# Multiplying the first two column tiles of the input projection together, feature tile by feature tile, with eight matmuls on zeros ahead

## The chip, the cores and the metric

The kernel runs on one core of a Trainium2 chip. The metric is the device time of one execution in microseconds (us). Besides the TensorE (PE in the profile; PEld is its weight load) a core has VectorE (DVE), ScalarE (ACT), GpSimd (POOL) and SyncE (SP), which here only issues DMAs. The engines run in parallel, each through its own list of instructions in order.

## What is computed

One layer of a hybrid decoder for 1024 positions of width 1024, in f32: RMSNorm, one input projection whose columns feed three kinds of token mixer (sparse attention, a gated convolution, gated linear attention), one output projection, a SwiGLU feed-forward part, a gated per-layer embedding, and a last norm. The part that the change touches is the projection, and of its columns the 512 of the convolution:

```
h = rms_norm(x, mix_norm_g[i])                      # x / rms(x) * g
z = h @ w_in[i]
(nq, kc, vc, ks_, vs_, kw, vw, ng, cu, gq, gk, gv, ga, gr) = jnp.split(z, split_at, axis=-1)
y_conv = conformer_conv(cu, ...)
def conformer_conv(u, w_dw, b_dw, ln_g, ln_b):
    a, g = jnp.split(u, 2, axis=-1)
    h = a * jax.nn.sigmoid(g)                       # then a causal convolution of 31 taps, norm, silu
```

## The kernel before

**Products.** TensorE computes in a shorter format than f32. Each f32 operand is therefore split into a high part (`hi`, written by ScalarE) and the rest (`lo`, written by VectorE or GpSimd), and each product is three matmuls: hi by hi, hi by lo, lo by hi.

**Operands of the projection.** `hT[hf][kt]` is the transposed input times the gain `g`, for half `hf` (512 positions) and feature tile `kt` (128 features, 8 tiles). `load_xT(hf)` loads 256 KB per tile and issues the two splitting instructions (L324 on ScalarE, L325 on VectorE). A tile of 128 output columns takes 512 KB of weights: `fetch(i)` calls `load_split`, one DMA into `nat` (L307), one cast into `whi` on ScalarE (L310) and one subtraction into `wlo` (L267). Here `whi` holds the eight 128x128 blocks of a column tile side by side.

**The tile product.** `mproj(i, hf, o)` goes over the eight feature tiles and issues the three matmuls of each (L368, L371, L372), 24 for one column tile and one half of the positions. `mtile(i)` does both halves, 48 matmuls, into two PSUM banks that the ring `early` gives out: tile 0 has banks 0 and 1, tile 1 banks 2 and 3, tile 2 banks 4 and 5, and tile 3 banks 0 and 1 again. So tile 3 has to wait until tile 0 has been read.

**What reads tile 0.** The norm's factor 1/rms per position is multiplied in after the product. `norm_x(hf)` loads x once more (8 loads of 512 KB), sums squares on ScalarE (L350), GpSimd forms the factors as diagonals `dg`, one matmul per half (L342) spreads them over the partitions, and ScalarE copies them into `rbc` (L343). Only then can VectorE read tile 0: `sg` = tile 0 by `rbc` (`scaled`, L355). `glu_tile(c)` goes on with a sigmoid of `sg` on ScalarE (L410, with a table load ahead), `sg` by `rbc` on GpSimd (L411), and `glu` = tile 1 by `sg` on VectorE (L414). The second call does the same with tiles 2 and 3. The taps of the convolution (L437, some 1.3 us each) follow on VectorE.

**After the four tiles** come row tiles: `row_tile` multiplies 128 positions by 384 columns of `w_a` (L398 to L400), then by 272 columns of `w_b`, for gated linear attention. Their weights pass through the same `load_split`. Later come tile 4, the chain of gated linear attention (`gla_ops`), attention, the output projection, and the feed-forward part.

**What sets the order.** The order in each engine's list is that of a scheduler which is given the program and simulates it with a cost table, and the places of the buffers in SBUF come from a dry pass of the same kind. So a change at the start can move instructions of any later part. SP issues a DMA only when the eighth DMA before it on SP has landed.

Of the kernel before, what the change touches and what calls it, by code (L numbers as in the profile page):

```python
# [10 lines left out]
F32R = mybir.dt.float32r  # L11
# [9 lines left out]
P = 128  # L21
NT = S // P
KT = D // P
# [195 lines left out]
def tile_block(ctx: ExitStack, tc: tile.TileContext, a: dict, out: bass.AP, plan: Plan):  # L219
    nc = tc.nc  # L220
    mm = nc.tensor.matmul
# [5 lines left out]
    banks = psum.tile([P, 8, 512], F32, name="banks")  # L227
# [11 lines left out]
    def B(name, dt=F32, shape=(P, 1024)):  # L239
        return place(name, shape, dt)  # L240
# [20 lines left out]
    low, high, early = Ring(0, 4), Ring(4, 8), Ring(0, 6)  # L261

    def f(ap):
        return ap.bitcast(F32)

    def sub(eng, o, i0, i1):
        return eng.tensor_tensor(out=o, in0=i0, in1=i1, op=ALU.subtract)  # L267
# [35 lines left out]
        return r  # L303

    def load_split(src, width=1024, lo_eng=None):
        nat = B("nat")
        nc.sync.dma_start(out=nat[:, :width], in_=src)  # L307
        hi = B("whi", F32R)
        lo_ = B("wlo", F32R)
        nc.scalar.copy(hi[:, :width], nat[:, :width])  # L310
        sub(lo_eng or nc.vector, lo_[:, :width], nat[:, :width], f(hi[:, :width]))
        return hi, lo_


    hT = [[], []]

    def load_xT(hf):
        for kt in range(KT):
            if kt % 2 == 0:
                xx = B("xT", F32, (P, 2, 512))  # L320
                for k in range(2):
                    nc.sync.dma_start(out=xx[:, k, :], in_=a["xT"][kt + k, :, hf * 512:hf * 512 + 512])
            x, o, g = xx[:, kt % 2, :], B("hT", F32R, (P, 2, 512)), pv["mixg"][:, kt:kt + 1]
            nc.scalar.activation(o[:, 0, :], x, AF.Copy, scale=g)  # L324
            nc.vector.scalar_tensor_tensor(out=o[:, 1, :], in0=x, scalar=g, in1=f(o[:, 0, :]), op0=ALU.mult,  # L325
                                           op1=ALU.subtract)
            hT[hf].append(o)
# [29 lines left out]
    ready = {}  # L357

    def fetch(i):
        if i < len(COL_T) and i not in ready:  # L360
            ready[i] = load_split(a["w_t"][i], lo_eng=nc.gpsimd if POOLLO[0] <= i < POOLLO[1] else None)

    def mproj(i, hf, o):
        hi, lo_ = ready[i]
        for kt in range(KT):
            w = slice(kt * P, (kt + 1) * P)
            x = hT[hf][kt]
            r = mm(o, hi[:, w], x[:, 0, :], start=kt == 0, stop=False)  # L368
            if kt == 0:
                behind("pe", r)  # L370
            mm(o, hi[:, w], x[:, 1, :], start=False, stop=False)  # L371
            mm(o, lo_[:, w], x[:, 0, :], start=False, stop=kt == KT - 1)  # L372

    def mtile(i):
        fetch(i)
        fetch(i + 1)
        ps = (early if i < 4 else low)(2)
        for hf in range(2):
            mproj(i, hf, ps[:, hf * 512:(hf + 1) * 512])
            for g, n in queue:  # L380
                pump(g, n)
        return ps
# [20 lines left out]

    glu = []

    def glu_tile(c):
        ps = mtile(2 * c)
        sg = B("sg")
        scaled(sg, ps)
        nc.scalar.activation(sg, sg, AF.Sigmoid)  # L410
        nc.gpsimd.tensor_tensor(out=sg, in0=sg, in1=rbc, op=ALU.mult)  # L411
        ps = mtile(2 * c + 1)
        h = B("glu")
        nc.vector.tensor_tensor(out=h, in0=ps, in1=sg, op=ALU.mult)  # L414
        glu.append(h)
# [84 lines left out]
        nc.scalar.activation(gr, pb[:, 16:272], AF.Silu, scale=rx[:, t:t + 1])  # L500
        nc.gpsimd.tensor_tensor(out=gr, in0=gr, in1=pv["gng"], op=ALU.mult)

    fetch(0)
    load_xT(0)
    fetch(1)
    load_xT(1)
    nc.sync.dma_start(out=cst[:, 0:P], in_=a["cst"][:, 0:P])
    fetch(2)
# [8 lines left out]
    wal = const.tile([17, P], F32, name="wal")  # L517
    nc.sync.dma_start(out=wal, in_=a["wal"])

    glu_tile(0)  # L520
    taps = conv_taps(0)
    pump(taps, 10)
    pump(loadA, 2)
# [14 lines left out]
    ps = mtile(4)  # L538
# [122 lines left out]
    for i in range(2):  # L661
        ps = mtile(5 + i)
# [54 lines left out]
    for t in range(NT):  # L717
        ps = row_tile(wV, 280, t)
# [871 lines left out]
```

## Time and profile before

| | |
|---|---|
| time, median of 3 runs (lowest to highest) | 1403.82 us (1403.34 to 1405.22) |
| the profiled execution: its time, its span | 1403.04 us, 1401.2 us |
| busy: PE, PEld | 1371.5 us (98%), 1160.7 us |
| busy: DVE, ACT, POOL | 1031.6 us (74%), 664.7 us (47%), 553.4 us (39%) |
| mean granted clock of TensorE | 0.995 of full |
| chain of work that ended last | PE 86%, DVE 7%, DMA 2% |

All times within the profile are counted from the start of the span. In an answer with instructions in order of time (a timeline) a row has its start, its duration, the engine, the source line, the operation, what it writes and reads, how many equal ones follow one another (x7), and in brackets how long the engine was idle ahead of it and what it waited for. Matmuls are pipelined, so that what one costs is the distance from its start to the next one's and not its duration.

### The profile page before, as it was taken

How to read it: one execution, taken by the hardware profiler on the slowest of the kernel's cores; microseconds unless marked ns; L12 is line 12 of the kernel's file. 1: busy time of each engine (PE TensorE's matmuls, PEld its weight loads, DVE VectorE, ACT ScalarE, POOL GpSimd, SP SyncE). 2: the span in 40 equal slices, each digit the busy share in tenths (PEclk: the TensorE clock that was granted, in tenths of full speed). 3: DMA queues.
4: the chain of work that ended last, by engine and by line, in shares of the span. 5: the costliest groups of instructions: out<-in, count | busy, mean ns of one | idle time of the engine just before them, and what ended most of it. 6: DMA issues, size and time to landing. Idle time of an engine off the chain costs nothing.

```text
span 1401.2 us, 19420 instructions
## 1 busy us (share of the span) xinstructions
PE 1371.5 (98%) x7080; PEld 1160.7 (83%) x7080; DVE 1031.6 (74%) x1870; ACT 664.7 (47%) x1290; POOL 553.4 (39%) x592
## 2 busy tenths in 40 slices
PE   8999999999999998999999999999999999999997
PEld 6898777889999997888878888888888788888886
DVE  3897457548999895558786777777789999897533
ACT  7331532246888885536433343333345344444532
POOL 3761443346888864101465665556510000000111
PEclk9999999999999999999999999999999999999999
DMA  9201013400000013541332222333357743521111
GB/s 362 75 16 40 11 54 102 148 23 4 6 9 5 5 33 107 181 149 40 120 113 92 81 99 102 109 113 113 105 194 264 259 152 111 178 78 66 69 39 46
DMA packets 55744, 135.68 MB, mean 97 GB/s; under 512 B 5413, under 2 KB 10207, under 8 KB 55647
## 3 DMA queue, kind: packets, MB, share of 16 engines
q1 hardware_dynamic: 55502, 134.42, 27.6%
q8 instruction: 55, 0.90, 0.3%
q14 instruction: 43, 0.34, 0.1%
q10 hardware_dynamic: 144, 0.01, 0.0%
HBM read 102.68 MB, written 31.73 MB: 96 GB/s over the span
## 4 chain that ended last, share of the span: by engine, by line
PE 86%; DVE 7%; DMA 2%; ACT 1%; issue 1%; POOL 1%; SPq 0%; POOLq 0%; DVEq 0%; ACTq 0%
PE banks L1435 13%; PE banks L1052 8%; PE banks L1051 8%; PE banks L1050 8%; PE banks L966 3%; PE banks L371 3%; PE banks L372 3%; PE banks L368 3%; PE banks L1010 2%; PE banks L1011 2%; PE banks L906 2%; PE banks L1151 2%; PE banks L1487 2%; PE banks L1486 2%; PE banks L1485 2%; PE banks L1152 2%
## 5 line engine op out<-in xcount | busy, mean ns | idle before, releaser
L1052 PE MATMUL banks<-op 128*128 128x512 f32 x616 | 237.8, 390 | 1.3 <-DVE op L267 1.3
L1051 PE MATMUL banks<-op 128*128 128x512 f32 x616 | 238.5, 390 | 0.0
L1050 PE MATMUL banks<-op 128*128 128x512 f32 x616 | 235.9, 390 | 0.6 <-ACT op L1039 0.3
L1435 PE MATMUL banks<-op 128*128 128x512 f32 x924 | 211.2, 389 | 2.5 <-ACT op L1039 1.7
L1435 PEld LDWEIGHTS banks<-op 128*128 128x128 f32 x924 | 173.2, 188 | 39.7 <-ACT op L1039 2.6
L1039 ACT CAST op<-nat 128x512 fp32r<-128x512 f32 x200 | 118.8, 621 | 180.4 <-DVE op L267 59.8
L267 DVE TENSOR_TENSOR op<-nat,op 128x512 fp32r<-128x512 f32 x196 | 152.7, 801 | 30.5 <-ACT op L1039 30.1
L301 POOL TENSOR_SCALAR rsr<-ss 128x1 f32<-128x1 f32 x16 | 5.9, 369 | 339.8 <-ACT sq L1454 261.9
L1052 PEld LDWEIGHTS banks<-op 128*128 128x128 f32 x616 | 115.6, 188 | 26.4 <-DVE op L267 2.1
L1050 PEld LDWEIGHTS banks<-op 128*128 128x128 f32 x616 | 115.6, 188 | 25.8 <-ACT op L1039 0.7
L1051 PEld LDWEIGHTS banks<-op 128*128 128x128 f32 x616 | 115.6, 188 | 24.2 <-issue 0.5
L267 DVE TENSOR_TENSOR op<-ws,op 128x512 fp32r<-128x512 f32 x88 | 88.0, 1004 | 52.5 <-ACT op L1039 52.4
L921 POOL TENSOR_SCALAR p<-p,sums,gates 128x640 f32<-128x640 f32 (+7 forms) x128 | 100.9, 801 | 39.3 <-DVE sums L917 30.2
L912 ACT ACTIVATE p<-p,mn 128x640 f32<-128x640 f32 (+7 forms) x128 | 94.7, 742 | 13.3 <-DVE mn L909 13.2
L368 PE MATMUL banks<-hT,whi 128*128 128x512 f32 x208 | 84.6, 407 | 7.0 <-ACT hT L324 6.4
L1039 ACT CAST op<-ws 128x512 fp32r<-128x512 f32 x88 | 54.4, 622 | 76.9 <-PE banks L1052 45.5
L371 PE MATMUL banks<-hT,whi 128*128 128x512 f32 x208 | 83.9, 403 | 0.5 <-DVE hT L325 0.5
L372 PE MATMUL banks<-hT,wlo 128*128 128x512 f32 x208 | 82.6, 399 | 0.0
L966 PE MATMUL banks<-cst,p 128*128 128x128 f32 x448 | 71.2, 274 | 1.9 <-DVE pt L267 0.9
L906 PE MATMUL banks<-k,qst 128*128 128x512 f32 (+2 forms) x192 | 68.3, 361 | 0.9 <-POOL qst L267 0.5
L267 DVE TENSOR_TENSOR pt<-banks,pt 128x512 fp32r<-128x512 f32 (+1 forms) x114 | 64.1, 571 | 5.6 <-ACT pt L977 4.8
L1344 DVE TENSOR_TENSOR x<-banks,x 128x512 f32<-128x512 f32 x96 | 64.3, 683 | 5.3 <-PE banks L1435 5.0
(305 smaller groups left out, 3309.6 us busy)
## 6 DMA issues: line engine op xcount, KB each, us to landing
nat<-actd SPq DMA_DIRECT2D x33, 512.0 KB, 5.4
nat<-in_w_g SPq DMA_DIRECT2D x22, 512.0 KB, 3.3
nat<-in_w_u SPq DMA_DIRECT2D x22, 512.0 KB, 3.2
nat<-in_w_d SPq DMA_DIRECT2D x22, 512.0 KB, 5.4
nat<-in_w_t SPq DMA_DIRECT2D x13, 512.0 KB, 4.2
actd<-sg SPq DMA_DIRECT2D x22, 256.0 KB, 2.4
actd<-sa SPq DMA_DIRECT2D x11, 512.0 KB, 2.8
actd<-sg SPq DMA_DIRECT2D x11, 512.0 KB, 3.7
```

The costliest lines, as they stand in the source:

```text
L267: return eng.tensor_tensor(out=o, in0=i0, in1=i1, op=ALU.subtract)
L368: r = mm(o, hi[:, w], x[:, 0, :], start=kt == 0, stop=False)
L371: mm(o, hi[:, w], x[:, 1, :], start=False, stop=False)
L372: mm(o, lo_[:, w], x[:, 0, :], start=False, stop=kt == KT - 1)
L906: mark("pe", mm(ps[:, :max(w, 256)], q, kdup[br][g][:, k], start=True, stop=False))
L921: nc.gpsimd.tensor_scalar(out=ps_out[br][:, :n], in0=ps_out[br][:, :n], scalar1=sums[:, br:br + 1], scalar2=gates[:, qb, 3 * head(h) + 1 + ...
L966: nc.tensor.transpose(ps[:, (2 * m + e) * P:(2 * m + e + 1) * P], blk(e, kb, br, ka), ident)
L1039: nc.scalar.copy(o[:, 0, :], src)
L1050: mm(ps, w[:, 0, c], x[k][:, 0, :], start=start and k == 0, stop=False, skip_group_check=True)
L1051: mm(ps, w[:, 0, c], x[k][:, 1, :], start=False, stop=False, skip_group_check=True)
L1052: mm(ps, w[:, 1, c], x[k][:, 0, :], start=False, stop=k == 3, skip_group_check=True)
L1435: mm(groups[g][t], r[:, v, c], l[:, u, :], start=start and (i, u, v) == (0, 0, 0), stop=i == len(ops) - 1 and u == 1, skip_group_check=True)
```

## The change

Ahead of all else VectorE clears a tile of 128x512 (`warm`) and TensorE multiplies it eight times with itself into bank 7, which nobody reads. The weights of column tiles 0 and 1 are loaded and split in three cuts each (256, 256 and 512 columns, that is 2, 2 and 4 feature tiles), issued in turns with the loads of the features; the first two feature tiles keep a load each, the others come two at a time (512 KB). `first_tiles` then goes over the feature tiles and issues for each the three matmuls of column tile 0 and the three of column tile 1, first for one half of the positions and then for the other; `glu_tile(0)` takes both.

```diff
+    def split_parts(src, parts, lo_eng=None):
+        nat, hi, lo_ = B("nat"), B("whi", F32R), B("wlo", F32R)
+        for c in parts:
+            nc.sync.dma_start(out=nat[:, c], in_=src[:, c])
+            nc.scalar.copy(hi[:, c], nat[:, c])
+            sub(lo_eng or nc.vector, lo_[:, c], nat[:, c], f(hi[:, c]))
+            yield hi, lo_
...
-    def load_xT(hf):
+    def load_xT(hf, part=None):
         for kt in range(KT):
+            if hf == 0 and kt in (0, 2, 4):
+                part(0)
             if kt % 2 == 0:
                 xx = B("xT", F32, (P, 2, 512))
-                for k in range(2):
-                    nc.sync.dma_start(out=xx[:, k, :], in_=a["xT"][kt + k, :, hf * 512:hf * 512 + 512])
+                if hf == 0 and kt == 0:
+                    for k in range(2):
+                        nc.sync.dma_start(out=xx[:, k, :], in_=a["xT"][kt + k, :, hf * 512:hf * 512 + 512])
+                        if k == 0:
+                            part(1)
+                else:
+                    if hf == 0 and kt < 6:
+                        part(1)
+                    nc.sync.dma_start(out=xx, in_=a["xT"][kt:kt + 2, :, hf * 512:hf * 512 + 512].rearrange("k p j -> p k j"))
...
-    def mproj(i, hf, o):
+    def mproj(i, hf, o, kts=range(KT)):
         hi, lo_ = ready[i]
-        for kt in range(KT):
+        for kt in kts:
...
+    def first_tiles():
+        two = [early(2) for _ in range(2)]
+        for hf in range(2):
+            for kt in range(KT):
+                for i in range(2):
+                    mproj(i, hf, two[i][:, hf * 512:(hf + 1) * 512], [kt])
+        return two
+
-    def glu_tile(c):
-        ps = mtile(2 * c)
+    def glu_tile(c, two=None):
+        ps = two[0] if two else mtile(2 * c)
...
-    fetch(0)
-    load_xT(0)
-    fetch(1)
+    warm = B("warm", F32R, (P, 512))
+    nc.vector.memset(f(warm), 0.0)
+    for _ in range(8):
+        mm(banks[:, 7, :], warm[:, :P], warm, start=True, stop=True)
+    cuts = [slice(0, 256), slice(256, 512), slice(512, 1024)]
+    w01 = [split_parts(a["w_t"][i], cuts) for i in range(2)]
+
+    def part(i):
+        ready[i] = next(w01[i])
+
+    load_xT(0, part)
     load_xT(1)
...
-    glu_tile(0)
+    glu_tile(0, first_tiles())
```

The scheduler also moves instructions around this part. In the changed kernel the lines stand further down: L368, L371 and L372 are L380, L383 and L384, L342 is L354, L343 is L355, L355 is L367, L414 is L435, L437 is L458.

On TensorE, at the end of tile 2, the second matmul on `dg` stood six matmuls ahead of tile 3 before:

```order
140 L342 MATMUL banks<-dg 128x512 [waits Pool_49]
141 L368 MATMUL banks<-hT,whi 128x512
142 L371 MATMUL banks<-hT,whi 128x512
143 L372 MATMUL banks<-hT,wlo 128x512
144 L368 MATMUL banks<-hT,whi 128x512
145 L371 MATMUL banks<-hT,whi 128x512
146 L372 MATMUL banks<-hT,wlo 128x512
147 L368 MATMUL banks<-hT,whi 128x512 [waits DVE_49]
```

Now, at the same place, where the last row is again the first matmul of tile 3:

```order
144 L380 MATMUL banks<-hT,whi 128x512
145 L383 MATMUL banks<-hT,whi 128x512
146 L384 MATMUL banks<-hT,wlo 128x512
147 L354 MATMUL banks<-dg 128x512 [waits Pool_49]
148 L380 MATMUL banks<-hT,whi 128x512 [waits DVE_49]
```

The six matmuls that lay between the `dg` matmul and the wait for VectorE's read of tile 0 are ahead of both.

On ScalarE, from the second copy into `rbc` on, before (the casts of 816 columns are those of `w_b`):

```order
37 L343 COPY rbc<-banks 128x512 [waits PE_49]
38 L410 ACT_TABLE_LOAD
39 L410 ACTIVATE sg<-sg 128x1024 [waits DVE_49] x2
40 L310 CAST whi<-nat 128x816 [waits DMAHW1_49,Activation_49]
41 L310 CAST whi<-nat 128x816 [waits DMAHW2_49,DVE_49]
```

and now:

```order
40 L355 COPY rbc<-banks 128x512 [waits PE_49]
41 L313 CAST whi<-nat 128x768 [waits DMAHW5_49,Activation_49]
42 L313 CAST whi<-nat 128x816 [waits DMAHW6_49,Pool_49]
43 L431 ACT_TABLE_LOAD
44 L431 ACTIVATE sg<-sg 128x1024 [waits DVE_49] x2
45 L313 CAST whi<-nat 128x816 [waits DMAHW7_49,Activation_49]
```

Two casts have come between the copy and the sigmoids. The one of 816 columns waits for the first DMA of `w_b`, and that DMA waits for a matmul two places ahead of the second `dg` matmul.

On VectorE, from the first `glu` to the second, before:

```order
26 L414 TENSOR_TENSOR glu<-banks,sg 128x1024 [waits Pool_49]
27 L425 TENSOR_SCALAR banks<-glu,par 128x1024 [waits DMAHW6_49,DVE_49]
28 L437 SCALAR_TENSOR_TENSOR banks<-glu,par,banks 128x1023 [waits DVE_49]
29 L437 SCALAR_TENSOR_TENSOR banks<-glu,par,banks 128x1022 [waits DVE_49]
30 L437 SCALAR_TENSOR_TENSOR banks<-glu,par,banks 128x1021 [waits DVE_49]
31 L267 TENSOR_TENSOR wlo<-nat,whi 128x816 [waits DMAHW2_49,PE_49,Activation_49]
32 L414 TENSOR_TENSOR glu<-banks,sg 128x1024 [waits PE_49,Pool_49]
```

and now:

```order
30 L435 TENSOR_TENSOR glu<-banks,sg 128x1024 [waits Pool_49]
31 L446 TENSOR_SCALAR banks<-glu,par 128x1024 [waits DMAHW3_49,DVE_49]
32 L267 TENSOR_TENSOR wlo<-nat,whi 128x816 [waits DMAHW7_49,Activation_49]
33 L458 SCALAR_TENSOR_TENSOR banks<-glu,par,banks 128x1023 [waits DVE_49]
34 L267 TENSOR_TENSOR wlo<-nat,whi 128x816 [waits DMAHW6_49,DVE_49]
35 L458 SCALAR_TENSOR_TENSOR banks<-glu,par,banks 128x1022 [waits DVE_49]
36 L458 SCALAR_TENSOR_TENSOR banks<-glu,par,banks 128x1021 [waits DVE_49]
37 L458 SCALAR_TENSOR_TENSOR banks<-glu,par,banks 128x1020 [waits DVE_49]
38 L435 TENSOR_TENSOR glu<-banks,sg 128x1024 [waits PE_49,Pool_49]
```

One more subtraction and one more tap have come between the two. The second `glu` reads tile 3, and the row tile that starts 32 matmuls after the end of tile 3 goes into a bank of tile 3, in both kernels: it waits for the second `glu`.

## Rows read from the trace of the kernel before

**Rows 1.** The page: busy time of TensorE and the others, share of span.

```profile
PE 1371.5 (98%) x7080; PEld 1160.7 (83%) x7080; DVE 1031.6 (74%) x1870; ACT 664.7 (47%) x1290; POOL 553.4 (39%) x592
```

**Rows 2.** Waits of TensorE: who waited for whom, total us, times, longest us.

```profile
PE banks L1005 <- DVE att L996: 2.9, 2, 2.7
PE banks L616 <- POOL kd L577: 1.0, 1, 1.0
```

**Rows 3.** Timeline of TensorE, the first matmuls.

```profile
6.42 0.80 PE L368 MATMUL banks<-hT,whi 128*128 128x512 f32 x1 [6.42 <-ACT hT L324]
7.72 0.79 PE L371 MATMUL banks<-hT,whi 128*128 128x512 f32 x1 [0.50 <-DVE hT L325]
8.31 0.63 PE L372 MATMUL banks<-hT,wlo 128*128 128x512 f32 x1
...
11.72 0.43 PE L371 MATMUL banks<-hT,whi 128*128 128x512 f32 x1
12.00 0.40 PE L372 MATMUL banks<-hT,wlo 128*128 128x512 f32 x1
```

**Rows 4.** Timelines of ScalarE and VectorE, the first splits.

```profile
4.70 1.04 ACT L310 CAST whi<-nat 128x1024 fp32r<-128x1024 f32 x1 [2.26 <-DMA nat<-in_w_t]
5.65 0.72 ACT L324 ACTIVATE hT<-xT,par 128x512 fp32r<-128x512 f32 x1
...
5.78 1.23 DVE L267 TENSOR_TENSOR wlo<-nat,whi 128x1024 fp32r<-128x1024 f32 x1 [5.78 <-ACT whi L310]
6.92 5.38 DVE L325 SCALAR_TENSOR_TENSOR hT<-xT,par,hT 128x512 fp32r<-128x512 f32 x8
```

**Rows 5.** Windows: busy us (instructions) of PE, PEld, DVE, ACT, POOL; PEclk; DMA share; GB/s.

```profile
3.00:12.00 9.00, 5.08 (x12) 3.65 (x13) 6.22 (x9) 6.49 (x10) 0.20 (x1) 1.00 1.00 375
```

**Rows 6.** Timeline of TensorE around the two dg matmuls and tile 3.

```profile
35.09 0.40 PE L371 MATMUL banks<-hT,whi 128*128 128x512 f32 x1
...
41.70 1.02 PE L342 MATMUL banks<-dg 128*128 128x512 f32 x2
...
44.66 0.50 PE L368 MATMUL banks<-hT,whi 128*128 128x512 f32 x1 [0.54 <-DVE sg L355]
```

**Rows 7.** Timelines of ScalarE, GpSimd and VectorE, from the sigmoids to the second glu.

```profile
42.76 0.59 ACT L343 COPY rbc<-banks 128x512 f32<-128x512 f32 x1 [3.05 <-PE banks L342]
43.36 1.28 ACT L410 ACT_TABLE_LOAD   x1
44.66 2.17 ACT L410 ACTIVATE sg<-sg 128x1024 f32<-128x1024 f32 x2
46.73 0.86 ACT L310 CAST whi<-nat 128x816 fp32r<-128x816 f32 x1
...
45.79 5.55 POOL L411 TENSOR_TENSOR sg<-sg,rbc 128x1024 f32<-128x1024 f32 x2 [5.23 <-ACT sg L410]
...
48.99 1.21 DVE L414 TENSOR_TENSOR glu<-banks,sg 128x1024 f32<-128x1024 f32 x1
...
51.63 3.93 DVE L437 SCALAR_TENSOR_TENSOR banks<-glu,par,banks 128x1023 f32<-128x1023 f32 x3
55.70 1.10 DVE L267 TENSOR_TENSOR wlo<-nat,whi 128x816 fp32r<-128x816 f32 x1
56.73 1.21 DVE L414 TENSOR_TENSOR glu<-banks,sg 128x1024 f32<-128x1024 f32 x1
```

**Rows 8.** Timeline of TensorE, the first matmuls of the row tiles.

```profile
55.67 0.33 PE L398 MATMUL banks<-whi,hT 128*128 128x384 f32 x1
...
63.84 0.33 PE L400 MATMUL banks<-whi,hT 128*128 128x384 f32 x1
```

**Rows 9.** DMA issues from 40 to 60 us: times issued, KB, us to landing.

```profile
nat<-in_w_b SPq DMA_DIRECT2D x1, 272.0 KB, 3.5
```

**Rows 10.** Timeline of GpSimd in gated linear attention.

```profile
160.88 0.19 POOL L301 TENSOR_SCALAR rsc<-bmv 128x1 f32<-128x1 f32 x1
161.15 0.57 POOL L302 TENSOR_TENSOR rsc<-rsc,mhalf 128x1 f32<-128x1 f32 x1
```

**Rows 11.** Windows around two later stretches, columns as in rows 5.

```profile
531.80:534.00 2.20, 0.05 (x1) 0.00 (x0) 1.12 (x4) 2.20 (x6) 2.20 (x3) 1.00 0.00 0
534.00:537.40 3.40, 2.88 (x12) 2.79 (x13) 3.37 (x6) 1.96 (x6) 3.40 (x3) 0.50 0.01 2
```

More of the change, by code (lines that the diff above doesn't have):

```diff
@@ L305, in load_split @@
     def load_split(src, width=1024, lo_eng=None):
[L306 to L312, printed above, removed]
+        return list(split_parts(src, [slice(0, width)], lo_eng))[-1]
+    def split_parts(src, parts, lo_eng=None):
[5 more added lines that the diff above has]
+            yield hi, lo_
     hT = [[], []]
-    def load_xT(hf):
+    def load_xT(hf, part=None):
         for kt in range(KT):
+            if hf == 0 and kt in (0, 2, 4):
+                part(0)
             if kt % 2 == 0:
                 xx = B("xT", F32, (P, 2, 512))
-                for k in range(2):
-                    nc.sync.dma_start(out=xx[:, k, :], in_=a["xT"][kt + k, :, hf * 512:hf * 512 + 512])
+                if hf == 0 and kt == 0:
[7 more added lines that the diff above has]
+                    nc.sync.dma_start(out=xx, in_=a["xT"][kt:kt + 2, :, hf * 512:hf * 512 + 512].rearrange("k p j -> p k j"))
             x, o, g = xx[:, kt % 2, :], B("hT", F32R, (P, 2, 512)), pv["mixg"][:, kt:kt + 1]
@@ L411, in glu_tile @@
         nc.gpsimd.tensor_tensor(out=sg, in0=sg, in1=rbc, op=ALU.mult)
-        ps = mtile(2 * c + 1)
+        ps = two[1] if two else mtile(2 * c + 1)
         h = B("glu")
```

## The prediction

> **What bounds the kernel now.** I read the busy times first: TensorE is busy in 98% of the span, no other engine in more than 74% [rows 1]. So time is gained where TensorE starts, waits or runs at its lower clock, and hardly elsewhere. Next the waits of TensorE: two to remember are that for GpSimd's `kd` in gated linear attention, 1.0 us, and the longest after the start, 2.7 us in attention [rows 2]. Then its first matmuls in order of time. The first starts at 6.42 us, the second waits 0.50 us for VectorE, and from 8.31 to 11.72 us eight matmuls follow one another at 3.41 / 8 = 0.426 us; at 12.00 us the twelfth starts [rows 3]. Later, from 35.09 to 41.70 us, 29 matmuls of the same shape take 6.61 us, 0.228 each [rows 6]: the first eleven ran at about half rate, the lower of the clock's two levels (1.2 and 2.4 GHz).
>
> The change can thus win at two places: the time before the first matmul, and 0.2 us on each slow one. What it wins there must then get past the next places where TensorE waits for others.
>
> **The start.** Before, the first high part of the features (L324) stands behind a cast of 1024 columns (1.04 us), the first low part behind a subtraction of 1.23 us [rows 4]. Now a quarter of each stands there. With a cut at 0.3 to 0.4 us the first product can start 0.7 to 0.9 us earlier; I take 5.6 us. Its first matmuls, two of them on the high part alone, still wait once for VectorE, so I let the third start at 6.25 us and the rest follow.
>
> Do the data keep up? Half 0 needs 1 MB of weights and 2 MB of features, 3.15 million bytes. From 3 to 12 us the DMAs moved 375 GB/s [rows 5], which brings these by 3.0 + 8.4 = 11.4 us. The last pair of feature tiles costs VectorE 1.34 us more (8 in 5.38 us [rows 4]), so it is ready at about 13.3 us; TensorE, if at full rate, comes to its first at 6.25 + 34 x 0.228 = 14.0 us. It keeps up with 0.7 us to spare, because each tile now feeds six matmuls where it fed three. The additional instructions (four casts and subtractions, a memset, eight matmuls that end near 4.6 us) lie in time in which their engines had nothing else.
>
> A rule speaks against cutting loads. The Trainium skill, "DMA: Bandwidth & Descriptors", section Bandwidth, wants DMAs of 1 MiB or more for three quarters of the peak. Loads of 256 and 512 KB, eight in flight, gave the 375 GB/s of the row here, so the trace bears it out badly; at three quarters of that rate the same bytes would come 2.8 us later and TensorE would wait some 2 us in half 0.
>
> What does the clock do? **Unknown: whether eight matmuls on zeros lift it.** The trace has no such matmuls. Bounds: the clock is up when the real work starts, or it rises at 11.8 us as before. At the slow rate they occupy TensorE for 8 x 0.426 = 3.4 us, the real work follows a microsecond later, and the rise of before came 5.4 us after its first matmul, 4.1 after its second. The two stretches together look to me like the busy time that was followed by the rise, so I take the upper case. At 12.00 us TensorE is then at matmul 3 + 5.75 / 0.228 = 28 instead of 12: **16 x 0.228 = 3.65 us ahead**. In the lower case, 24 matmuls that would have started by 11.8 us are 12, and 2.6 us of that are gone.
>
> The Trainium skill, "TensorE: Matmul & The Clock Gate", Part 1, calls the slow state the default, which activity ends, and says that the number of slow matmuls at a start differs from run to run. No run here shows the second; it would put single runs between the two cases.
>
> **Tile 3.** The work up to the second `dg` matmul is else the same, but six matmuls that stood behind it are now ahead [the order rows of TensorE above]. Before, from the start of this matmul to the start of tile 3 went 44.66 - 41.70 = 2.96 us [rows 6]: spread, copy into `rbc` (42.76, 0.59), VectorE's read. These steps stay as they are, and cover is gone: the six, 1.36 us, are no longer hidden in it. Second `dg` matmul at 39.4 us (41.70 - 3.65 + 1.36), tile 3 at 42.36. **Lead left: 2.3 us.** GpSimd's `dg` cannot spoil it by much: squares and factors hang on the loads of x, whose bytes come as before, and 41.70 left them several us.
>
> **The second glu.** Here I expect most of the loss. ScalarE's sigmoids now stand behind the cast of the first `w_b` piece. Its DMA waits for a matmul 0.45 us ahead of the second `dg` matmul, 38.95 us. Its landing: one of 272 KB took 3.5 us among few others [rows 9]; this one has 408 KB and the DMAs to itself, and I take the same, thus 42.5, where the copy into `rbc` (1.65 us behind the `dg` matmul, as before) and the other cast are done at 41.9. Cast 0.86, table load 1.30, sigmoid 1.09, GpSimd's multiply 2.78 (5.55 for two) [rows 7] make 48.5 us for the first `glu`; before it was 48.99. Of the 2.3 us of lead only 0.5 have come through. From the first to the second `glu` went 56.73 - 48.99 = 7.74 us; one subtraction (1.10) and one tap (3.93 / 3 = 1.31) more stand between, 10.15. It starts at 58.7 and ends at 59.9 (1.21). TensorE needs this 32 matmuls behind tile 3: tile 3 ends 55.67 - 44.66 = 11.0 us after its start, at 53.4, and 32 at (63.84 - 55.67) / 47 = 0.174 [rows 8] make 58.9. **New wait: 1.0 us; lead left 1.3.** Before there was none: 55.67 + 5.6 = 61.2, against 57.9. What is queued behind it are the other row tiles, which would have been early by as much. Bounds: 0.4, if the DMA has landed by 41.9, and 2.3, if it takes over a microsecond longer than I say.
>
> **Gated linear attention.** GpSimd now does a pair on `rsc` (0.19 + 0.57 [rows 10]) ahead of its eight multiplies of `qb` and of `kd`, for which TensorE waited 1.0 us already. **0.76 us more**, between 0 (GpSimd was idle ahead of `qb`, and the pair may fit there) and 1.5.
>
> VectorE's taps in between don't count: a subtraction in them now waits for a late DMA, some 2 us, but VectorE was idle for 4.5 us behind its taps before it had to read tile 4. Attention and the output projection have a few other places in the order; I have no row that prices them, and the bounds are a wait of [rows 2] more or less. The feed-forward part has the same order.
>
> **Sum:** -3.65 + 1.36 + 1.0 + 0.76 = -0.53 us against the profiled 1403.04 (a span of 1401.2 and 1.8 around it), which is 0.8 below the median of the runs. Against the median: 1403.3. 0.2% of this is 2.8 us, which is about what a measurement of this kernel can tell from no change.
>
> **The rivals.**
>
> *The lead survives* (0.28). The `w_b` piece lands in time and `rsc` fits into GpSimd's idle time. Then 2.3 - 0.4 = 1.9 us stay: 1401.9 us, or down to 1400.9 where the first product also starts earlier than I say and some of VectorE's steps behind the first `glu` are quicker. For it: DMAs are few at 40 us. Against it: the DMA is issued only 3 us ahead of where its cast would have to start.
>
> *A wait of attention goes* (0.10). At 531.8 us TensorE is idle for 2.2 us and more, and behind this runs 3.4 us at a granted clock of 0.50 [rows 11], 1.7 us lost. If another order or a small shift removes both, 4.4 us are gained: 1399.4. Nothing in the change aims there.
>
> *The zeros don't lift the clock* (0.14). Then the work is done in the changed order at the slow rate up to 11.8 us, as if the warm matmuls weren't there: the lead is 1.05 - 1.36 = -0.3 at tile 3, and the waits behind it, which are counted from the second `dg` matmul, move along: 1403.3 + 2.6 = 1405.9.
>
> *The slower side: new idle time lets the clock fall* (0.10). Ahead of tile 3 TensorE now has nothing for 2.96 - 1.0 = 1.9 us, where it was idle for 0.54 [rows 6], and 1.0 us at the second `glu`. An idle time of 0.54 left the clock up; the one at 531.8, of 2.2 to 2.7 us, was followed by half rate [rows 2, 11]. It decides somewhere between. A drop of 3.4 us costs 1.7, which gives 1405.0; at both places 3.4: 1406.7.
>
> **How the numbers follow.** The forecast, a lead earned and spent, has 0.38, the rivals 0.28, 0.10, 0.14 and 0.10. The likeliest case alone lies in 1402.2 to 1404.6. For 8 in 10 I leave out the wait of attention below and the double drop of the clock above, and reach to a lead that survives almost whole, 1400.8, and somewhat past zeros that do nothing, 1406.4. Faster by over 0.2%, below 1401.0, is the wait of attention and 0.12 of the surviving lead, where other small waits go with it: 0.22. Slower, above 1406.6, is 0.07 of the last rival and 0.08 of the one on zeros, where a new wait in the moved order comes on top: 0.15. The rest is no change, 0.63.
>
> **What would show it.** The first real matmul at 5.4 to 5.9 us, and the third and later ones at 0.228 us, not 0.426. The second `dg` matmul near 39.4, tile 3 near 42.4, with an idle time ended by VectorE's `sg`. On ScalarE an idle time ahead of a cast of 816 columns that a DMA of `w_b` ends. A wait of TensorE for `glu` near 59 us, and a wait for `kd` of over 1 us near 160. The forecast is wrong if that wait for `glu` is missing, if matmuls at 0.426 reach to 11 us, or if a stretch behind 300 us has changed by more than the start has.

## The result, and the profile after

The changed kernel takes 1412.14 us (median of 6 runs, 1410.65 to 1415.74) where the kernel before took 1404.51 (6 runs beside them, 1401.22 to 1405.68): a ratio of 1.0064 (95% interval 1.0049 to 1.0078), 9 us slower by the ratio, and outside the forecast range. The profiled execution took 1413.79 us, with a span of 1412.0.

The busy time of TensorE and its waits, from the page and the view of waits (total us, times, longest):

```profile
PE 1380.1 (98%) x7088; PEld 1166.7 (83%) x7088; DVE 1035.3 (73%) x1875; ACT 665.9 (47%) x1294; POOL 551.9 (39%) x592
```
```profile
PE banks L410 <- DVE glu L435: 2.7, 1, 2.7
...
PE banks L380 <- ACT hT L336: 2.1, 1, 2.1
...
PE banks L380 <- DVE sg L367: 1.9, 1, 1.9
```

TensorE's busy time has risen by 8.6 us against [rows 1] for eight more matmuls of 0.43 us. So besides waits there is slower running. To see where, I follow one and the same matmul through the traces: its start is read in each, and the difference is how late TensorE stands there.

| start of | before | changed | later by |
|---|---|---|---|
| tile 3 | 44.66 | 45.76 | 1.10 |
| fifth row tile on `w_b` (its first L398) | 101.02 | 106.64 | 5.62 |
| first L748, key compression | 268.73 | 273.99 | 5.26 |
| first L1151, output projection | 537.10 | 543.54 | 6.44 |
| first L1050, feed-forward part | 638.56 | 646.38 | 7.82 |
| end of span | 1401.2 | 1412.0 | 10.8 |

More than half is there by 107 us. The first matmuls, in order of time:

```profile
1.43 3.78 PE L528 MATMUL banks<-warm 128*128 128x512 f32 x8 [1.43 <-DVE warm L526]
5.01 0.63 PE L380 MATMUL banks<-hT,whi 128*128 128x512 f32 x1
...
7.63 0.40 PE L380 MATMUL banks<-hT,whi 128*128 128x512 f32 x1
7.87 0.40 PE L384 MATMUL banks<-hT,wlo 128*128 128x512 f32 x1
...
9.03 0.39 PE L384 MATMUL banks<-hT,wlo 128*128 128x512 f32 x1
11.51 0.73 PE L380 MATMUL banks<-hT,whi 128*128 128x512 f32 x2 [2.09 <-ACT hT L336]
```

The first product comes at 5.0 us, earlier than the 5.6 of the forecast, and full spacing begins at 7.6, where the forecast had 6.25. The twelfth matmul starts at 9.03 us and not at 12.00 [rows 3], a lead of 3.0 us. Then TensorE stands still for 2.09 us, for the third feature tile, whose split on ScalarE itself waits for a load, and the next matmul, the thirteenth, leads by only 0.7 us (11.51 against 12.23):

```profile
10.73 1.33 ACT L336 ACTIVATE hT<-xT,par 128x512 fp32r<-128x512 f32 x2 [3.32 <-DMA xT<-in_xT]
```

Windows of the changed kernel (columns as in rows 5): from 3 to 12 us the DMAs moved 296 GB/s against 375 in [rows 5], and further down the five later stretches in which TensorE worked at a granted clock of 0.50:

```profile
3.00:12.00 9.00, 6.63 (x20) 4.29 (x18) 3.54 (x7) 4.12 (x9) 0.00 (x0) 1.00 0.87 296
65.50:68.80 3.30, 3.30 (x12) 3.30 (x11) 3.26 (x4) 0.00 (x0) 3.30 (x3) 0.50 0.26 66
297.60:304.30 6.70, 6.70 (x22) 5.47 (x22) 2.20 (x11) 3.81 (x12) 3.26 (x6) 0.50 0.00 0
461.40:464.70 3.30, 3.30 (x14) 3.11 (x14) 1.91 (x5) 0.16 (x1) 1.47 (x2) 0.50 0.00 0
539.90:546.70 6.80, 5.74 (x19) 4.97 (x20) 5.19 (x9) 3.55 (x9) 5.25 (x4) 0.50 0.00 1
1106.60:1109.80 3.20, 3.20 (x9) 2.42 (x9) 3.20 (x7) 0.62 (x1) 0.00 (x0) 0.50 1.04 401
```

The kernel before has such stretches only at 534 to 537 us [rows 11] and at 292 to 298:

```profile
291.70:298.50 6.80, 6.80 (x25) 5.86 (x25) 2.79 (x16) 4.44 (x13) 2.46 (x5) 0.50 0.00 0
```

In the changed one they add up to 24 us instead of 10, and half of the difference, some 7 us, is lost. The slow matmuls at the start are no part of this: there the column of the granted clock reads 1.00 in both kernels, also while matmuls follow one another at 0.426 us [rows 3, rows 5], so what is said here of the clock at the start is read from the spacing alone.

The largest new wait, from the `dg` matmul to the row tile, in the timelines of TensorE, ScalarE and VectorE:

```profile
42.81 1.02 PE L354 MATMUL banks<-dg 128*128 128x512 f32 x2
45.76 0.50 PE L380 MATMUL banks<-hT,whi 128*128 128x512 f32 x1 [1.93 <-DVE sg L367]
...
65.20 0.51 PE L410 MATMUL banks<-whi,hT 128*128 128x384 f32 x1 [2.68 <-DVE glu L435]
65.50 0.52 PE L411 MATMUL banks<-wlo,hT 128*128 128x384 f32 x1
...
68.95 0.34 PE L410 MATMUL banks<-whi,hT 128*128 128x384 f32 x1
69.12 0.33 PE L411 MATMUL banks<-wlo,hT 128*128 128x384 f32 x1
```
```profile
45.90 0.88 ACT L313 CAST whi<-nat 128x816 fp32r<-128x816 f32 x1 [0.72 <-DMA nat<-in_w_b]
```
```profile
51.65 1.23 DVE L435 TENSOR_TENSOR glu<-banks,sg 128x1024 f32<-128x1024 f32 x1 [3.95 <-POOL sg L432]
...
54.16 1.75 DVE L267 TENSOR_TENSOR wlo<-nat,whi 128x816 fp32r<-128x816 f32 x1
...
57.04 3.14 DVE L267 TENSOR_TENSOR wlo<-nat,whi 128x816 fp32r<-128x816 f32 x1
60.10 3.92 DVE L458 SCALAR_TENSOR_TENSOR banks<-glu,par,banks 128x1022 f32<-128x1022 f32 x3
63.92 1.22 DVE L435 TENSOR_TENSOR glu<-banks,sg 128x1024 f32<-128x1024 f32 x1
```

From 62.5 to 65.2 us TensorE waits for the second `glu`, and right behind it the matmuls follow at 0.32 us instead of 0.17 until 68.9: the granted clock has fallen to 0.50. The wait of 2.7 us and the some 1.7 that the slow stretch costs are, together, nearly all of the 4.5 us by which TensorE falls back between tile 3 and 107 us.

### The profile page after: what moved, and what is told of

It is laid out like the page before. It is cut to its first block, busy times and chain, and to the rows that moved or that the text cites. A ratio compares the mean times of both kernels' runs of the same rounds, so it can differ in the third digit from the quotient of the medians.

```text
span 1412.0 us, 19441 instructions
## 1 busy us (share of the span) xinstructions
PE 1380.1 (98%) x7088; PEld 1166.7 (83%) x7088; DVE 1035.3 (73%) x1875; ACT 665.9 (47%) x1294; POOL 551.9 (39%) x592
## 4 chain that ended last, share of the span: by engine, by line
PE 82%; DVE 9%; DMA 3%; ACT 2%; issue 2%; POOL 1%; SPq 0%; POOLq 0%; DVEq 0%; ACTq 0%
PE banks L1465 12%; PE banks L1082 8%; PE banks L1081 8%; PE banks L1080 8%; PE banks L996 3%; PE banks L383 3%; PE banks L384 3%; PE banks L380 3%; PE banks L1040 2%; PE banks L1041 2%; DVE op L267 2%; PE banks L936 2%; PE banks L1181 2%; PE banks L1183 2%; PE banks L1182 2%; PE banks L937 2%
## 5 line engine op out<-in xcount | busy, mean ns | idle before, releaser
L942 ACT ACTIVATE p<-p,mn 128x640 f32<-128x640 f32 (+7 forms) x128 | 94.7, 742 | 13.2 <-DVE mn L939 13.1
L380 PE MATMUL banks<-hT,whi 128*128 128x512 f32 x208 | 82.2, 403 | 4.3 <-ACT hT L336 2.1
L383 PE MATMUL banks<-hT,whi 128*128 128x512 f32 x208 | 83.9, 403 | 0.1
L384 PE MATMUL banks<-hT,wlo 128*128 128x512 f32 x208 | 82.5, 398 | 0.0
```

## The experiments

Each is told against runs of the kernel before on the same chip (medians 1403.0 to 1403.7 us).

**Zeros alone (warm_only).** The kernel before, with these lines ahead and the order else the same:

```diff
+    warm = B("warm", F32R, (P, 512))
+    nc.vector.memset(f(warm), 0.0)
+    for _ in range(8):
+        mm(banks[:, 7, :], warm[:, :P], warm, start=True, stop=True)
     fetch(0)
     load_xT(0)
```

> The kernel before, with the memset and the eight matmuls on zeros ahead and nothing else; the order of all other instructions is that of the kernel before. Theory A (the zeros lift the clock early, and what the changed kernel loses is lost by the loads and the moved order): matmuls at 0.228 us from 7 to 8 us on, the first tile then bound by the low parts of the features, tile 3 near 42.8 us instead of 44.66, no new wait behind it, a time 1 to 2.5 us below that of the kernel before. Theory B (a lead at the start is taken away by the waits of later stages, whatever the loads are): tile 3 as early, but the time within 0.7 us of before. Theory C (the matmuls on zeros are harmful in themselves, by the bank, the memset or the clock falling again): slower than before.

Measured: 1404.76 us (12 runs), ratio 1.0012 (0.9997 to 1.0027). No gain, and at the start none was possible in the profiled execution, since the full spacing began later than without zeros [rows 3]. It was the slowest of the twelve (1409.83 us); how the others started is not on record. Its matmuls:

```profile
12.83 0.56 PE L371 MATMUL banks<-hT,whi 128*128 128x512 f32 x1
13.23 0.40 PE L372 MATMUL banks<-hT,wlo 128*128 128x512 f32 x1
13.46 0.39 PE L368 MATMUL banks<-hT,whi 128*128 128x512 f32 x1
```

None of the three theories had such a late rise. Tile 3 starts at 45.23, 0.57 later than before.

**Eleven zeros (warm_11)**, `range(11)` in the same lines, so that no gap is left ahead of the first product:

> The kernel before with eleven matmuls on zeros instead of eight, which reach to 6.1 us, where the first product starts; order else as before. Theory D (eight didn't lift the clock because about a microsecond without work lay between them and the first product): the clock is up by 8.5 us, matmuls at 0.228 from there, tile 3 at 43 to 43.7, the time 0.5 to 1.5 us below that with eight. Theory E (where the clock rises is chance from run to run, zeros or not): a rise anywhere from 6 to 13 us, and a median within 0.7 us of the kernel before.

Measured: 1406.2 us (12 runs), ratio 1.0021 (1.0001 to 1.004). In its profile full spacing begins at 8.1 us and TensorE is 1.5 us ahead at 30 us, as D has it. But the order was not wholly that of before: the second `dg` matmul came directly ahead of tile 3, as in the changed kernel, and 1.93 us of waiting for `sg` took the lead away (tile 3 at 44.53).

**No zeros (no_warm)**, the changed kernel without the four lines above:

> The changed kernel without the memset and the matmuls on zeros; the order of the rest is that of the changed kernel. Theory A: the clock rises between 9 and 12 us; since the features are late anyway, TensorE waits for the third feature tile until about 11.5 us with or without the zeros, so that tile 3 starts at 45.8 to 47, the wait for the second glu of 2 to 3 us is still there, and the time is 1410 to 1414, within 2 us of the changed kernel. If instead the zeros carry what the change wins, it is 3 us or more slower than the changed kernel.

Measured: 1410.47 us (11 runs), ratio 1.004 (1.0026 to 1.0054): no slower than with zeros (1.0064 and 1.0051 in its two measurements). Without them TensorE runs at half rate until 9.5 us, and still comes to the missing feature tile early:

```profile
9.52 0.39 PE L384 MATMUL banks<-hT,wlo 128*128 128x512 f32 x1
11.32 0.73 PE L380 MATMUL banks<-hT,whi 128*128 128x512 f32 x2 [1.42 <-ACT hT L336]
```

Tile 3 starts at 45.62 against 45.76. In these profiles, what the clock gives ahead of the missing tile is waited away at it. Here the clock fell behind the wait of 1.93 us ahead of tile 3 (0.50 from 47.0), and the wait for the second `glu` was then 0.97 us.

**Features one by one (no_pairs)**, the cuts left; the order of the engines other than SP is that of the changed kernel but for a few rows of TensorE (shortened):

```diff
-                    nc.sync.dma_start(out=xx, in_=a["xT"][kt:kt + 2, :, hf * 512:hf * 512 + 512].rearrange("k p j -> p k j"))
+                    for k in range(2):
+                        nc.sync.dma_start(out=xx[:, k, :], in_=a["xT"][kt + k, :, hf * 512:hf * 512 + 512])
```

> The changed kernel with the features loaded one tile at a time (256 KB) as before, the cuts of the weights kept; the order on ScalarE, VectorE and GpSimd is that of the changed kernel. Theory A1 (small cuts slow the loads): from 4 to 8 us still under 280 GB/s, the third feature tile split near 9 to 10 us, the fourth near 11, an idle time of TensorE of 0.5 to 2 us there. Theory A2 (the pair of 512 KB, which counts as landed only when all of it is there, delays the third tile): third tile split by 8 us and no idle time over 0.3 us. Behind it the wait for the second glu as in the changed kernel, so a time of 1409 to 1413 by either.

Measured: 1407.64 us (10 runs), ratio 1.0033 (1.0019 to 1.0047). ScalarE splits the third tile at 7.32 us, without a wait, where it was 10.73:

```profile
7.32 0.72 ACT L334 ACTIVATE hT<-xT,par 128x512 fp32r<-128x512 f32 x1
9.06 0.72 ACT L334 ACTIVATE hT<-xT,par 128x512 fp32r<-128x512 f32 x1 [1.02 <-DMA xT<-in_xT]
```

No long wait is left at the start, tile 3 starts at 43.33, 2.4 us earlier than in the changed kernel. A2 holds for the place: it was the pair. That it was the landing of both halves together, and not a slower transfer of the pair, is argued and not shown. The rate from 4 to 8 us is 290 GB/s, above the 280 of A1, yet below the 358 of the kernel before; no_cuts below, with the pairs kept and no cuts, has 364 from 3 to 12 us where the changed kernel has 296, so the cuts cost rate as well. The wait for the second `glu` is there unchanged (2.7 us), and the clock falls behind it. By the two ratios the time is 4.4 us below the changed kernel, which neither theory expected.

**Two cuts (two_cuts)**, `cuts = [slice(0, 512), slice(512, 1024)]`. The scheduler gives this kernel another order, in gated linear attention above all:

> The changed kernel with two cuts of 512 columns (256 KB, rows of 2 KB) in place of three. Half a megabyte more stands ahead of the second pair of features than with three cuts. Theory A1 (small cuts with rows of 1 KB slow the loads): 300 GB/s or more from 4 to 8 us, and the second pair split by 10 us, no later than with three cuts in spite of more bytes ahead. If rows of 1 KB don't matter, it comes 1 to 1.5 us later than with three cuts, near 12 us.

One run, 1397.97 us. 261 GB/s from 4 to 8 us, below the 300 of A1, and the second pair at 10.83, between the two cases: whether the rows of 1 KB matter stays open. More runs of it are told below.

**w_b behind (glu_first)**, casts and subtractions of `w_b` held back (`behind` adds an order on the engine, no wait):

```diff
-        nc.scalar.activation(sg, sg, AF.Sigmoid)
+        r = nc.scalar.activation(sg, sg, AF.Sigmoid)
+        if c == 0:
+            mark("sg", r)
...
-        nc.vector.tensor_tensor(out=h, in0=ps, in1=sg, op=ALU.mult)
+        r = nc.vector.tensor_tensor(out=h, in0=ps, in1=sg, op=ALU.mult)
+        mark("glu", r)
...
-            nc.scalar.copy(hi[:, c], nat[:, c])
-            sub(lo_eng or nc.vector, lo_[:, c], nat[:, c], f(hi[:, c]))
+            r = nc.scalar.copy(hi[:, c], nat[:, c])
+            if late:
+                behind("sg", r)
+            r = sub(lo_eng or nc.vector, lo_[:, c], nat[:, c], f(hi[:, c]))
+            if late:
+                behind("glu", r)
...
```

`late` is set for the loads of `w_b` alone.

> The changed kernel, with w_b's casts held behind the first sigmoid on ScalarE and w_b's subtractions behind the second glu on VectorE; all else stands in the order of the changed kernel. Theory A: start and tile 3 as in the changed kernel (45.8), the first glu 1.6 us earlier (near 50), the second ending near 58.5 to 60 instead of 65.1, the wait of 2.7 us at the row tile gone and with it the 3.4 us at half rate behind it, so that TensorE is 4 to 4.5 us earlier by 80 us; the time 3.5 to 5 us below the changed kernel, 1407 to 1409. If the loss lies in later stages instead, the time moves by less than 2 us.

Measured: 1406.47 us (12 runs), ratio 1.0018 (1.0005 to 1.0031), 0.46% or 6.5 us below the changed kernel by the two ratios. VectorE:

```profile
51.12 1.23 DVE L441 TENSOR_TENSOR glu<-banks,sg 128x1024 f32<-128x1024 f32 x1 [2.37 <-POOL sg L438]
...
53.77 6.57 DVE L465 SCALAR_TENSOR_TENSOR banks<-glu,par,banks 128x1023 f32<-128x1023 f32 x5
60.25 1.22 DVE L441 TENSOR_TENSOR glu<-banks,sg 128x1024 f32<-128x1024 f32 x1
```

From the first `glu` to the second 9.13 us instead of 12.27, the wait gone, no stretch at half rate there, and TensorE 3.5 us earlier at the fifth row tile on `w_b` (103.18 against 106.64), although tile 3 started 1.05 later than in the changed kernel: the wait for the third feature tile was 3.0 us here, and the clock fell behind it (0.50 from 11 to 15 us; tile 3 at 46.81). Of the two causes taken out one at a time, here and in no_pairs, this one gives back more.

**Both orders (both_orders)**: this, and the six matmuls put back:

```diff
-        mm(ps, dg[:, 512:640], dg[:, :512], start=True, stop=True)
+        mark("dg", mm(ps, dg[:, 512:640], dg[:, :512], start=True, stop=True))
...
+            if (i, hf, kt) == (2, 1, 6):
+                behind("dg", r)
```

> The changed kernel with both order repairs: w_b behind the sigmoid and the second glu, and six matmuls of tile 2 put back behind the second dg matmul. The loads in cuts and pairs stay. Theory A: the features still come late (an idle time of 1.5 to 3 us near 9 to 11.5 us), the second dg matmul near 41.4, tile 3 at 44.2 to 45 instead of 45.8, no wait for the second glu, the time 1 to 1.5 us below the run with the first repair alone, 1404 to 1406, still not below the kernel before, because the late features have eaten the lead. If the late features didn't matter, the time would be 1401 to 1403.

Measured: 1405.03 us (12 runs), ratio 1.0013 (0.9998 to 1.0028). Second `dg` matmul at 40.99, tile 3 at 43.95, the wait for `sg` 0.54 us again, that for the third feature tile still 2.2 us, as theory A has it.

**Whole loads (no_cuts)**, `cuts = [slice(0, 1024)]`, two DMAs of 512 KB. The scheduler then puts the `dg` matmul and the sigmoids where they were before, by itself:

> The changed kernel with the weights of tiles 0 and 1 loaded whole (two DMAs of 512 KB in place of six), the rest of its code the same; the scheduler then also puts the sigmoids ahead of the casts of w_b and six matmuls behind the second dg matmul again, as in the kernel before. Theory A: the first product about 1 us later (near 6 us), the second pair of feature tiles split by 9.5 us instead of 12, the idle time of 2.1 us near 9 to 11.5 us gone, tile 3 at 42 to 43.5, no wait for the second glu, and a time of 1401 to 1404, below the kernel before. Theory B (later stages take it away, or the order in which two tiles are multiplied costs by itself): 1404 to 1408.

Measured: 1404.15 us (12 runs), ratio 1.0002 (0.9987 to 1.0016). 364 GB/s from 3 to 12 us, no wait of 2 us, none for the second `glu`; the loss is gone, but theory A's gain isn't there. Full spacing began at 11 us in its profile, the first product came at 6.26, and tile 3 waits 1.30 us for `sg`, to 44.96.

**All three causes out (repaired)**: both orders, features one by one, cuts, zeros and tile by tile order kept:

> The changed kernel with the three causes taken out together: w_b behind the sigmoid and the second glu, six matmuls behind the second dg matmul, features loaded one tile at a time; the cuts, the zeros and the tile by tile order stay. Theory A: no idle time over 0.5 us between 6 and 12 us, tile 3 near 42 us (44.66 before), no wait for the second glu, TensorE 2 to 2.7 us ahead of the kernel before from 60 to 140 us, of which gated linear attention takes up to 1; a time 2 to 3 us below the run with the two order repairs, 1401.5 to 1403, and 0.5 to 2.5 below the kernel before. Rival (a lead at the start doesn't reach the end, whatever makes it): within 0.7 us of the kernel before.

Measured: 1404.98 us (11 runs), ratio 1.0007 (0.9994 to 1.002). Tile 3 at 43.14, no wait over 0.9 us up to 120 us, TensorE 1.52 us ahead of the kernel before at the fifth row tile on `w_b` (99.50), 0.91 ahead at L748 (267.82), still 0.95 at 337 us, and 0.65 behind at the output projection (537.75): 0.6 us go by the end of gated linear attention, and a stretch at half rate from 455.8 us that the kernel before does not have takes 1.7. A second one, from 534.3 us, is twice as long as before. The rival holds for the time: this lead didn't reach the end.

**Two cuts, more runs (two_cuts_timed):**

> The kernel with two cuts of 512 columns again, now timed. Its one run so far took 1398.0, with tile 3 1.2 us later than in the kernel before, and its gain came between 140 and 300 us, where the scheduler has put gated linear attention and the first part of attention in another order, and one stretch at half rate was missing. If the order makes the gain, the median is 1398 to 1401. If the missing stretch was chance, 1400 to 1404.

Measured: 1400.86 us (12 runs), ratio 0.9982 (0.9969 to 0.9994): faster than both kernels. Tile 3 starts at 45.63, later than before by 1.0, L748 at 263.95, earlier by 4.8. TensorE's waits from 120 to 300 us, all of them:

```profile
PE banks L646 <- ACT yT L677: 0.5, 1, 0.5
PE banks L673 <- POOL m L669: 0.2, 1, 0.2
```

In the kernel before the same stretch has 4.1 us, with the 1.0 for `kd` of [rows 2]:

```profile
PE banks L707 <- ACT gates L726: 1.3, 1, 1.3
...
PE banks L620 <- DVE gst L624: 0.8, 1, 0.8
PE banks L906 <- POOL qst L267: 0.5, 1, 0.5
PE banks L616 <- ACT yT L647: 0.5, 1, 0.5
```

So, by its place, it is the scheduler's other order, 100 us behind the changed lines, that wins, and not the start. No run takes this order without the cuts or the cuts without this order.

**Two cuts with features one by one (two_cuts_no_pairs), and without zeros (two_cuts_no_warm)**, in the order of two_cuts but for a few rows:

> Two cuts of 512 columns, and the features loaded one tile at a time; the order on ScalarE, VectorE and GpSimd is that of the kernel with two cuts, on TensorE too but for two rows. Theory A: the idle time ahead of the third feature tile (2.4 us in one profile of two cuts, 0.2 in the other, where the clock rose late) is gone, tile 3 at 43 to 44.5 instead of 45.6 to 45.9; since this order had no wait for the second glu and its gain lies between 140 and 300 us, the lead adds to it, and the median is 1398.5 to 1400, that is 1 to 2.5 us below two cuts with pairs. Rival (a lead at the start doesn't reach the end): TensorE is ahead by 1.5 us or more at 100 us, by less than 0.5 us at 250, and the median is within 0.7 us of that with pairs.

> Two cuts of 512 columns without the memset and the matmuls on zeros; order of the rest the same. If the zeros lift the clock early in most runs and this counts, the median is 1 us or more above that with zeros. If the wait for the features hides it, and the place of the rise is chance, it is within 0.7 us.

Measured: 1399.95 us (ratio 0.9978, 0.9968 to 0.9988) and 1399.35 us (0.9978, 0.9966 to 0.9991), 12 runs each. Features one by one: tile 3 at 44.20, 1.4 earlier than in two_cuts_timed, and this lead is still there at L748 (262.54 against 263.95) and at the feed-forward part (631.39 against 633.44). So in these two profiles the lead reaches that far. The median is only 0.9 lower, which the intervals don't tell from 0. Without zeros two_cuts is no slower.

**The changed kernel again (changed_again):**

> The changed kernel itself, for a second profile. If the wait of 2.7 us for the second glu is one of its order, it is there again, whether or not the clock falls behind it; the stretches at half rate that followed no such wait (near 461 and 1106 us) may be missing. Median 1410 to 1413.

Measured: 1411.22 us (4 runs), ratio 1.0051 (1.0035 to 1.0068). The same waits (2.5 us for the third feature tile, 2.2 for `sg`, 2.5 for `glu`), and the clock at 0.50 behind the last:

```profile
65.20:68.40 3.20, 3.11 (x10) 3.11 (x11) 3.17 (x5) 0.00 (x0) 3.07 (x3) 0.50 0.16 19
```

The fifth row tile on `w_b` starts at 106.68, 5.66 us later than in the kernel before, as in the first profile. The stretches at half rate at 461 and 1106 us are missing.

## Why the prediction was wrong

**"It keeps up with 0.7 us to spare" failed.** The step took 375 GB/s from a row in which the loads were of 256 and 512 KB, took for granted that bytes are worth the same when they come as a pair, and asked only when the last pair would be there. Measured was 240 GB/s from 4 to 8 us, and the third tile, asked for together with the fourth in 512 KB, was split at 10.73 us: 2.09 us of waiting (2.5 in the second profile), most of the lead. With the clock up later than I took it (full spacing from 7.6 us and not from 6.25), 0.25 us of the 3.65 is left at the second `dg` matmul (42.81, less the 1.36 of the six moved ones, against 41.70), and tile 3 starts at 45.76 instead of 42.36. With the tiles one by one, the cuts and the zeros kept, the wait is gone. Against this I had set a rule of the Trainium skill, "DMA: Bandwidth & Descriptors", section Bandwidth, and worked out "some 2 us" of waiting from it, an estimate to which I gave too little weight; its size fits, its reason only in part, since no_pairs lost the wait with more and smaller DMAs.

**"New wait: 1.0 us" was the right place and under half the size.** The mechanism is shown, by glu_first: w_b's cast ahead of the sigmoids, its subtractions between the two `glu`. From the `dg` matmul to the first `glu` I had 9.1 us, measured 8.8; from the first to the second 10.15, measured 12.27. The term that was mis-sized is the two subtractions at 1.10 us each [rows 7]; they took 1.75 and 3.14. The wait was 2.68. The second one starts just behind the start of an addition on GpSimd for its own taps (56.98 us, 2.33 long), and ends 0.87 us after it; in the kernel before only 0.23 us of that addition were left at the start of the subtraction, so the price read there didn't hold here.

**The clock behind it was a rival at 0.10 and happened**, in both profiles of the changed kernel, at the second `glu`: some 4.4 us for wait and slow stretch where the sum had 1.0. Where the wait is taken out (glu_first, both_orders, repaired) no such stretch comes at this place.

**Right were** the missing cover of six matmuls (2.95 us from the `dg` matmul to tile 3, where I had 2.96, and both_orders gives back 1.4 us of waiting), and the order of size in gated linear attention (0.6 us of the lead in repaired; in the changed kernel itself there was no loss, since it came late: TensorE waited 0.6 us for `kd`, not more than the 1.0 before).

**The zeros**: the unknown was taken at its upper end, the clock up when the work starts. In the twelve profiles with zeros full spacing begins between 4.8 us, with the first product (glu_first), and 13.2 us (warm_only), in nine of them by 8.1 us; in the three without zeros at 9.5 us, 10.9 and, in the kernel before, 12.0. So with them it mostly begins earlier, but not in every execution. That it varies is what the Trainium skill, "TensorE: Matmul & The Clock Gate", Part 1, says of the number of slow matmuls; the runs agree. No pair of kernels that differ in the zeros alone shows a gain from them. For the changed kernel the profiles show why: TensorE then waits for the third feature tile. For warm_only, where the slowest execution is the one that was profiled, it stays open.

**Past 107 us the sum had only the 0.76 us of gated linear attention**, and there the loss is 5.2 us in one profile of the changed kernel and 1.0 in the other. It lies in stretches at half rate that come and go between executions of one kernel. The mean granted clock of every execution is on record and gives an estimate of what they cost: the span times what is missing to 1 (the slow start isn't in it, and some 2 us of it fall at the end of the span, where TensorE has no more work). The ten executions of the changed kernel have 0.989 to 0.993 and lose 12.4 us in the mean; 109 of the kernel before have 0.991 to 0.997, median 0.995, and lose 6.8. So of the 8.5 us by which the mean spans differ 5.6 are half rate, where the known stretch behind the second `glu` is 1.7, and it is no chance of one profile. The remaining 2.9 us are waits, work and the slow start.

The same numbers say where the gain of the other kernels went. Without the time lost at half rate no_cuts is 1.8 us shorter than the kernel before, and it loses 2.6 us more there; repaired is 0.5 shorter, which the spread doesn't tell from 0, and loses 2.2 more; two_cuts_timed is 4.6 shorter and loses 2.0 more. The moved order isn't needed for this: warm_only, in the order of the kernel before, loses 9.4 us against 6.8, and in its profile has stretches at 456 and 1102 us where the changed kernel has its own at 461 and 1106. Why all these kernels fall to half rate more often stays open.

## What to carry to other kernels

Work that is moved to start earlier is only as early as its last input: follow each load to the instruction that waits for it, with the loads in the size and number in which they will now be issued. Look past the edit in each engine's order for what now stands ahead of a long chain (here one cast on ScalarE and two subtractions on VectorE), and hold such work behind the chain. A difference of a few us that a scheduler's new order makes 100 us further on can outweigh the edit, so an edit is judged by the order that comes with it. And split a difference into what the granted clock took and the rest before explaining it: here no_cuts had less of the rest and was still no faster.

## What the runs showed of the hardware

- A wait of TensorE can cost more than itself: behind waits of 1.9 to 3.0 us its granted clock fell to 0.50 in some executions (no_warm behind 1.93, the changed kernel behind 2.68 and 2.5, glu_first behind 3.0), and not in others (the changed kernel behind the 1.93 ahead of tile 3, and behind the 2.09 and 2.5 for the third feature tile).
- A subtraction of 816 columns on VectorE took 1.10 us in one place and 3.14 in another. In the slow case GpSimd ran an operation on two tensors for 2.33 us in the same time:

```profile
56.98 2.33 POOL L455 TENSOR_TENSOR part<-ptmp,part 128x995 f32<-128x995 f32 x1
```

  In 14 of the 15 profiles an 816-column subtraction starts while such an addition on GpSimd runs, and each time it takes what is left of the addition plus 0.85 to 0.87 us: 0.23 left and 1.10 (before), 0.30 and 1.17 (glu_first), 1.45 and 2.32 (two_cuts), 1.63 and 2.48 (both_orders), 2.27 and 3.14 (changed). That the subtraction waits for the addition to end fits all 14; no run moves the addition alone.
- Ten loads of 128, 256 and 512 KB, issued within 5 us in the changed kernel, moved 240 GB/s from 4 to 8 us where loads of 256 and 512 KB moved 358 in the same four microseconds of the kernel before.
